# A two-layer decoder step on one NeuronCore: the queries' 1/rms multiplied into the low-rank rows, query evictions on ScalarE, four heads in turn

## Chip, core and metric

The kernel runs on one core of one Trainium2 chip. The metric is the device time of one execution in microseconds (us), the median of several runs; lower is better. The kernel before takes 2415.44 us (three runs, 2413.04 to 2415.65).

## What is computed

One inference step of a decoder of two layers, in float32, for 1024 prompt tokens and 64 sample tokens (8 sequences of 8), 1088 columns in all. The first layer mixes tokens by causal means. The second is attention with a compressed latent of 256 numbers and a rotary key of 64 per token. Each layer then has an MLP with squared ReLU and a gated add. The part that the change touches is how the queries of the second layer are made:

```python
def _rmsnorm(x, g):
    xf = x.astype(jnp.float32)
    y = xf * lax.rsqrt(jnp.mean(xf * xf, axis=-1, keepdims=True) + NORM_EPS)
    return (y * g.astype(jnp.float32)).astype(x.dtype)

def _mla_queries(u, pos, w_dq, q_norm, w_uq, w_uk):
    cq = _rmsnorm(u @ w_dq, q_norm)              # 384 numbers per token
    q = jnp.einsum('btr,rhe->bthe', cq, w_uq)    # 8 heads x (128 + 64)
    q_lat = jnp.einsum('bthn,rhn->bthr', q[..., :QK_NOPE], w_uk)
    return q_lat, _rope(q[..., QK_NOPE:], pos)
```

The factor 1/rms ("rstd") is one number per token. It can be multiplied into `cq` ahead of the product with `w_uq`, or into the product after it.

## The kernel before

Activations lie transposed, features on the 128 partitions and tokens along the columns, in three chunks of columns: chunk 0 and chunk 1 with 384 tokens, chunk 2 with 320 (256 prompt tokens and the 64 sample tokens). A float32 product is made of three matmuls: each operand is split into a rounded high half (a cast, on ScalarE, L146) and the remainder (a subtraction on VectorE, L147), and `mm3` (L188 to L190) adds high x high, high x low and low x high in one PSUM bank.

The order of the program is a list of steps that `Plan` collects and then runs; `add_late(n, fn)` puts a step behind the next n steps that use a weight piece. The weight pieces are loaded ahead on SP's queue (L168) through a ring of four. Each engine works through its own instructions in the order in which they are built, so an instruction that waits holds up all that stand behind it on its engine; a scheduler in the compiler may interleave neighbouring steps.

The stages are: pooling, first MLP, first gated add, `qkv_phase` (L662), attention, output projection, second MLP, second gated add. The change lies in `qkv_phase`, which works as follows.

- `krope` and `latent` make the rotary key and the latent of the three chunks.
- `qdown(c)` (L747) makes the 384 low-rank query rows of chunk c, three PSUM banks of 24 matmuls each; `split_scaled` multiplies by the gain of the norm and splits them. The squares are added up in the tile `acc` (L259).
- `low_rstd(c)` (L687) turns the sums of squares into the two rstd rows of a chunk, that of the latent and that of the queries: two matmuls with a column of ones (L694) give a row in PSUM, ScalarE copies it (L696), a DMA folds it over the partitions (L697, `ss`), VectorE finds 1/sqrt by three Newton steps (L699 to L705), a DMA writes the row to DRAM (L709, `row`), and a second one reads it back to all 128 partitions (L710, into `E["r"]`, a slab whose tile is called `hid`).
- `latent_end(c)` (L720) multiplies the latent by its rstd, stores and splits it.
- `qrope(g, c)` (L772) makes the rotary part of four heads from two banks of 9 matmuls each, with six VectorE operations (L781), two casts (L794) and two subtractions; four stores go to DRAM (L799, `q_d`). For g = 0 a step ahead of these multiplies the cosine and sine tables of the chunk by the queries' rstd (L784), so that the rotary part is scaled with them.
- `qnope(hh, c)` (L758) makes the other part of head hh from one bank of 9 matmuls. VectorE evicts it and multiplies by the rstd at once (L762), and SP stores it (L764, `qn_d`). In chunk 2 ScalarE copies the sample tokens aside (L768).

The heads come in pairs: heads 0 and 1 of all chunks, then 2 and 3, and so on; ahead of every fourth `qnope` stands one `qrope`. The attention that follows makes values and keys (tiles `vh`, `kh`, `one`), loads the queries back (L168 `raw<-qn_d`, L178 `q<-q_d`) and starts with the scores (L891, tile `s`).

Of the kernel before, what the change touches and what calls it, by code (L numbers as in the profile page):

```python
# [11 lines left out]
F32 = mybir.dt.float32  # L12
F32R = mybir.dt.float32r
I32 = mybir.dt.int32
AF = mybir.ActivationFunctionType
ALU = mybir.AluOpType
# [4 lines left out]
P = 128  # L21
# [23 lines left out]
CH = [(0, 384), (384, 384), (768, 320)]  # L45
NCH = len(CH)
# [66 lines left out]
def kernel(ctx: ExitStack, tc: tile.TileContext, io: dict):  # L113
    nc = tc.nc
# [15 lines left out]
    def gain(name):  # L130
        o, w = io["gain_at"][name]
        return gains[:, o:o + w]

    h = []
    qn_d = [dpool.tile([P, T], F32, name=f"qn_d{i}") for i in range(H)]
# [9 lines left out]
    def split(hi, lo, x):  # L145
        nc.scalar.copy(out=hi, in_=x)  # L146
        nc.vector.tensor_tensor(out=lo, in0=x, in1=hi.bitcast(F32), op=ALU.subtract)  # L147

    def split_scaled(hi, lo, x, g):
        nc.scalar.activation(hi, x, AF.Copy, scale=g)  # L150
        nc.vector.scalar_tensor_tensor(  # L151
            out=lo, in0=x, scalar=g, in1=hi.bitcast(F32), op0=ALU.mult, op1=ALU.subtract)
# [27 lines left out]
    plan = Plan(load_piece)  # L180
# [32 lines left out]
    def u_pair(c):  # L213
        n = CH[c][1]
        uh = S["u"].tile([P, n], F32R, tag=f"uh{c}", bufs=KT, name="uh")
        ul = S["u"].tile([P, n], F32R, tag=f"ul{c}", bufs=KT, name="ul")
        return uh, ul

    def slab():
        return S["hid"].tile([P, 2176], F32R, tag="hid", bufs=5, name="hid")  # L220
# [29 lines left out]
    def square(c, x, acc, add=None, new=None):  # L250

        n = CH[c][1]
        if acc is None:
            acc = S["tmp"].tile([P, n], F32, tag=f"acc{c}", bufs=1, name="acc") if new is None else new()
            nc.scalar.activation(acc, x, AF.Square)
        else:
            s = sq_tile(n)
            nc.scalar.activation(s, x, AF.Square)  # L258
            (add or nc.vector).tensor_tensor(out=acc, in0=acc, in1=s, op=ALU.add)  # L259
        return acc  # L260
# [57 lines left out]
    def lin(c, w, k, m, mo, src=None):  # L318
        n = CH[c][1]
        wh, wl = (x.rearrange("p (k m) -> p k m", k=k) for x in w)  # L320
        ps = bank()[:, :n]
        x = src or U[c]
        mm3(ps, [(wh[:, i, mo:mo + m], wl[:, i, mo:mo + m], x[i][0], x[i][1]) for i in range(k)])
        return ps
# [337 lines left out]
    def qkv_phase():  # L662
        E = {}
# [20 lines left out]
        def hl_tile(n):  # L684
            return S["hl"].tile([P, 384], F32, tag="hl", bufs=4, name="hl")[:, :n]

        def low_rstd(c):  # L687

            o, n = CH[c]
            p, m = small_shape(c)  # L690
            ss = tiny("ss", (p, 2 * m)).rearrange("p (k m) -> p k m", k=2)
            for k, (name, dim) in enumerate((("zz", KR), ("qq", QR))):
                ps = bank()[0:1, :n]
                nc.tensor.matmul(out=ps, lhsT=ones, rhs=E[name, c], start=True, stop=True)  # L694
                row = sq_tile(n)[0:1]
                nc.scalar.activation(row, ps, AF.Copy, scale=1.0 / dim)  # L696
                nc.scalar.dma_start(out=ss[:, k, :], in_=row)  # L697
            q = RC[c].unsqueeze(1).broadcast_to([p, 2, m])
            nc.vector.tensor_tensor(out=ss, in0=ss, in1=q, op=ALU.mult)  # L699
            nc.vector.tensor_tensor(out=ss, in0=ss, in1=q, op=ALU.mult)  # L700
            v = ss.rearrange("p k m -> p (k m)")
            nc.vector.tensor_scalar(out=v, in0=v, scalar1=EPS, scalar2=None, op0=ALU.add)
            y = rsqrt(v).rearrange("p (k m) -> p k m", k=2)
            nc.vector.tensor_tensor(out=y[:, 0], in0=y[:, 0], in1=RC[c], op=ALU.mult)
            nc.vector.scalar_tensor_tensor(  # L705
                out=y[:, 1], in0=y[:, 1], scalar=SCALE, in1=RC[c], op0=ALU.mult, op1=ALU.mult)
            row = dpool.tile([2, n], F32, name=f"row{S['rows']}")
            S["rows"] += 1
            nc.sync.dma_start(out=row.rearrange("k (p m) -> p k m", p=p), in_=y)  # L709
            nc.sync.dma_start(out=E["r"][:, :, o:o + n], in_=row.partition_broadcast(P))  # L710
# [9 lines left out]
        def latent_end(c):  # L720
            o, n = CH[c]
            r = E["r"][:, 0, o:o + n]
            g = gain("kv_norm")
            for i in range(2):
                z = E["z"][:, i, o:o + n]
                nc.vector.scalar_tensor_tensor(
                    out=z, in0=z, scalar=g[:, i:i + 1], in1=r, op0=ALU.mult, op1=ALU.mult)
                nc.sync.dma_start(out=io["latT"][i, :, o:o + n], in_=z)
                split(*[x[:, o:o + n] for x in S["cl"][i]], z)
# [17 lines left out]
        def qdown(c, *ws):  # L747
            pss = [lin(c, w, KT, P, 0) for w in ws]
            g = gain("q_norm")
            out = []  # L750
            for i, ps in enumerate(pss):
                uh, ul = u_pair(c)
                split_scaled(uh, ul, ps, g[:, i:i + 1])
                out.append((uh, ul))
                E["qq", c] = square(c, ps, E.get(("qq", c)))
            E["cq", c] = out

        def qnope(hh, c, w):  # L758
            o, n = CH[c]
            ps = lin(c, w, 3, P, (hh % 2) * P, E["cq", c])  # L760
            t = hl_tile(n)
            nc.vector.tensor_tensor(out=t, in0=ps, in1=E["r"][:, 1, o:o + n], op=ALU.mult)  # L762
            m = min(n, SEQ - o)
            nc.sync.dma_start(out=qn_d[hh][:, o:o + m], in_=t[:, :m])  # L764
            if m < n:
                if hh % 4 == 0:
                    E["qs"] = S["hl"].tile([P, 4, NS], F32, tag="qs", bufs=2, name="qs")
                nc.scalar.copy(out=E["qs"][:, hh % 4, :], in_=t[:, m:])  # L768
                if hh % 4 == 3:
                    nc.sync.dma_start(out=qns_d[hh // 4], in_=E["qs"])  # L770

        def qrope(g, c, w):  # L772

            o, n = CH[c]
            pss = [lin(c, w, 3, P, i * P, E["cq", c]) for i in range(2)]
            s = slab()[:, :5 * n].rearrange("p (k t) -> p k t", k=5)
            _, _, z1, t, x2 = (s[:, i, :].bitcast(F32) for i in range(5))
            cos, sin = (E["cs"][:, i, o:o + n] for i in range(2))

            def tt(out, a, b, op):  # L780
                nc.vector.tensor_tensor(out=out, in0=a, in1=b, op=op)  # L781

            if g == 0:
                nc.vector.tensor_tensor(  # L784
                    out=E["cs"][:, :, o:o + n], in0=E["cs"][:, :, o:o + n],
                    in1=E["r"][:, 1, o:o + n].unsqueeze(1).broadcast_to([P, 2, n]), op=ALU.mult)
            tt(z1, pss[0], cos, ALU.mult)
            tt(t, pss[1], sin, ALU.mult)
            tt(z1, z1, t, ALU.subtract)
            tt(t, pss[0], sin, ALU.mult)  # L790
            tt(x2, pss[1], cos, ALU.mult)
            tt(x2, x2, t, ALU.add)
            for z, hi in ((z1, 1), (x2, 3)):
                nc.scalar.copy(out=s[:, hi, :], in_=z)  # L794
                tt(s[:, hi + 1, :], z, s[:, hi, :].bitcast(F32), ALU.subtract)
            m = min(n, SEQ - o)
            v = s[:, 1:5, :].bitcast(F32)
            for i in range(4):
                nc.sync.dma_start(  # L799
                    out=q2_d[4 * g + i][:, o:o + m].rearrange("(q p) t -> p q t", q=4),  # L800
                    in_=v[32 * i:32 * i + 32, :, :m])
            if m < n:
                nc.sync.dma_start(out=qs_d[:, g * P:(g + 1) * P, :].rearrange("q p t -> p q t"), in_=v[:, :, m:])
# [7 lines left out]
        for c in range(NCH):  # L811
            plan.add(lambda *w, c=c: qdown(c, *w), *dq)
            plan.add_late(min(c + 1, 2), lambda c=c: low_rstd(c))
            plan.add_late(9, lambda c=c: latent_end(c))
        ropes = [(g, c) for g in range(2) for c in range(NCH)]
        nopes = [(hh, c) for j in range(4) for c in range(NCH) for hh in (2 * j, 2 * j + 1)]
        for i, (hh, c) in enumerate(nopes):
            if i % 4 == 0:
                g, cc = ropes.pop(0)
# [470 lines left out]
    mlp_phase(0)  # L1290
    ple_phase(0, lambda c: next_norm(c, None))
    qkv_phase()
    attention_phase()
    wo_phase()
# [124 lines left out]
```

## Time and profile before

| | us |
|---|---|
| median of three runs | 2415.44 |
| the profiled execution, its own time | 2413.58 |
| its span, first to last instruction | 2411.8 |
| TensorE (PE) busy | 2361.0 |
| VectorE (DVE) busy | 1226.1 |
| ScalarE (ACT) busy | 829.4 |
| mean granted TensorE clock, as a share of 2.4 GHz | 0.992 |

The profile page gives busy time by engine, the chain of work that ended last, and groups of instructions by source line. Matmuls overlap, so a busy PE says little of how fast it goes; gaps between the starts of matmuls, and the granted clock, say more. The part that the change touches runs from about 970 to 1097 us of the span, the attention from there to about 1410.

### The profile page before, as it was taken

Reading aid. Unit: us, or ns where it says so; the run is one execution under the profiler, and the core shown is the slowest. Engines: PE = TensorE matmul, PEld = TensorE weight load, DVE = VectorE, ACT = ScalarE, POOL = GpSimd, SP = SyncE. Lnnn points to the kernel's source line nnn. Section 1 sums busy time; section 2 is a strip of 40 time slices with the busy share of each in tenths; the row PEclk is TensorE's granted clock in tenths of the full one; section 3 lists DMA queues with packets and bytes.
Section 4 is the critical chain, followed back from the end, with each engine's and each line's share of the span. In section 5 each row is a group of like instructions: output and inputs, shape, how many; then the busy total and the mean of one; then the engine's idle time right before and its main releaser. Section 6 shows DMA issues by size and latency. Waiting matters only on the chain.

```text
span 2411.8 us, 35848 instructions
## 1 busy us (share of the span) xinstructions
PE 2361.0 (98%) x14516; PEld 2308.6 (96%) x14516; DVE 1226.1 (51%) x2406; ACT 829.4 (34%) x1557; POOL 11.0 (0%) x16
## 2 busy tenths in 40 slices
PE   7999999999999999998999999999999999999996
PEld 7999999999999999987988899999999999999996
DVE  5933333333333578477887765433333333334755
ACT  6622121121221444236777644312212212123432
POOL 0000000000000000000000000000000000000001
PEclk8999999999999999999999999999999999999998
DMA  8411111111111143257443351111111111111202
GB/s 269 125 55 44 44 45 44 44 44 47 49 47 44 40 124 130 58 153 223 149 126 125 94 200 55 52 47 49 44 44 44 44 44 44 44 44 44 64 27 78
DMA packets 97085, 186.53 MB, mean 77 GB/s; under 512 B 18633, under 2 KB 69001, under 8 KB 96144
## 3 DMA queue, kind: packets, MB, share of 16 engines
q1 hardware_dynamic: 90535, 179.78, 23.9%
q10 hardware_dynamic: 6384, 4.47, 0.6%
q8 instruction: 114, 1.87, 0.3%
q14 instruction: 52, 0.42, 0.1%
HBM read 155.00 MB, written 28.85 MB: 76 GB/s over the span
## 4 chain that ended last, share of the span: by engine, by line
PE 89%; DVE 4%; DMA 3%; ACT 2%; issue 1%; SPq 1%; ACTq 0%; DVEq 0%
PE mm L188 27%; PE mm L190 27%; PE mm L189 27%; PE s L891 2%; PE one L941 1%; PE one L1006 1%; PE one L918 1%; DMA craw<-in_cache 1%; PE mm L468 1%; ACT p L899 0%; PE mm L269 0%; DVE mx L898 0%; DVE hid L781 0%; PE one L188 0%; DMA hid<-row 0%
## 5 line engine op out<-in xcount | busy, mean ns | idle before, releaser
L188 PE MATMUL mm<-uh,whi 128*128 128x384 f32 (+1 forms) x2460 | 806.8, 328 | 12.8 <-ACT whi L146 5.9
L190 PE MATMUL mm<-uh,wlo 128*128 128x384 f32 (+1 forms) x2460 | 804.9, 327 | 0.2 <-DVE wlo L147 0.2
L189 PE MATMUL mm<-ul,whi 128*128 128x384 f32 (+1 forms) x2460 | 804.6, 327 | 0.0
L190 PE MATMUL mm<-hid,wlo 128*128 128x384 f32 (+1 forms) x1584 | 517.3, 327 | 0.0
L188 PE MATMUL mm<-hid,whi 128*128 128x384 f32 (+1 forms) x1584 | 517.1, 326 | 0.0
L189 PE MATMUL mm<-hid,whi 128*128 128x384 f32 (+1 forms) x1584 | 516.7, 326 | 0.0
L188 PEld LDWEIGHTS mm<-uh,whi 128*128 128x128 f32 x2460 | 464.0, 189 | 21.7 <-ACT whi L146 6.1
L190 PEld LDWEIGHTS mm<-uh,wlo 128*128 128x128 f32 x2460 | 463.9, 189 | 0.7 <-DVE wlo L147 0.7
L189 PEld LDWEIGHTS mm<-ul,whi 128*128 128x128 f32 x2460 | 464.0, 189 | 0.3 <-DVE ul L147 0.3
L146 ACT CAST whi<-raw 128x1024 fp32r<-128x1024 f32 (+3 forms) x184 | 190.9, 1038 | 753.1 <-PE mm L189 740.3
L314 DVE TENSOR_TENSOR h<-h,mm 128x384 f32<-128x384 f32 (+1 forms) x408 | 216.3, 531 | 422.2 <-PE mm L190 418.3
L188 PEld LDWEIGHTS mm<-hid,whi 128*128 128x128 f32 x1584 | 297.3, 188 | 3.8 <-issue 3.8
L190 PEld LDWEIGHTS mm<-hid,wlo 128*128 128x128 f32 x1584 | 297.3, 188 | 0.0
L189 PEld LDWEIGHTS mm<-hid,whi 128*128 128x128 f32 x1584 | 297.2, 188 | 0.0
L147 DVE TENSOR_TENSOR wlo<-raw,whi 128x1024 fp32r<-128x1024 f32 (+3 forms) x184 | 222.0, 1207 | 78.1 <-ACT whi L146 78.0
L557 DVE SCALAR_TENSOR_TENSOR t<-mm,r 128x384 f32<-128x384 f32 (+1 forms) x192 | 102.6, 535 | 299.4 <-PE mm L190 299.4
L559 ACT ACTIVATE t<-t 128x384 f32<-128x384 f32 (+1 forms) x192 | 97.0, 505 | 390.0 <-DVE t L557 390.0
L147 DVE TENSOR_TENSOR hid<-t,hid 128x384 fp32r<-128x384 f32 (+1 forms) x192 | 102.4, 534 | 140.4 <-ACT hid L146 140.4
L258 ACT ACTIVATE sq<-h 128x384 f32<-128x384 f32 (+1 forms) x126 | 63.2, 505 | 121.4 <-DVE h L314 60.2
L146 ACT CAST hid<-t 128x384 fp32r<-128x384 f32 (+1 forms) x192 | 95.0, 495 | 6.0
L259 DVE TENSOR_TENSOR acc<-acc,sq 128x384 f32<-128x384 f32 (+1 forms) x132 | 71.8, 544 | 42.3 <-ACT sq L258 41.5
L151 DVE SCALAR_TENSOR_TENSOR ul<-h,gains,uh 128x384 fp32r<-128x384 f32 (+1 forms) x96 | 54.0, 592 | 4.3 <-ACT uh L150 4.3
(206 smaller groups left out, 1944.6 us busy)
## 6 DMA issues: line engine op xcount, KB each, us to landing
raw<-in_w_up SPq DMA_DIRECT2D x64, 512.0 KB, 3.4
raw<-in_w_down SPq DMA_DIRECT2D x64, 512.0 KB, 3.5
craw<-in_cache SPq DMA_DIRECT2D x64, 192.0 KB, 2.7
raw<-in_w_gate SPq DMA_DIRECT2D x16, 512.0 KB, 3.5
craw<-in_cache SPq DMA_DIRECT2D x64, 128.0 KB, 2.1
h<-in_x_prompt SPq DMA_DIRECT2D x8, 512.0 KB, 6.7
raw<-qn_d SPq DMA_DIRECT2D x8, 512.0 KB, 3.5
q<-q_d SPq DMA_DIRECT2D x8, 512.0 KB, 4.8
```

Of the source, the lines that this page charges most:

```text
L146: nc.scalar.copy(out=hi, in_=x)
L147: nc.vector.tensor_tensor(out=lo, in0=x, in1=hi.bitcast(F32), op=ALU.subtract)
L151: nc.vector.scalar_tensor_tensor(out=lo, in0=x, scalar=g, in1=hi.bitcast(F32), op0=ALU.mult, op1=ALU.subtract)
L188: nc.tensor.matmul(out=out, lhsT=wh, rhs=xh, start=i == 0, stop=False)
L189: nc.tensor.matmul(out=out, lhsT=wh, rhs=xl, start=False, stop=False)
L190: nc.tensor.matmul(out=out, lhsT=wl, rhs=xh, start=False, stop=i == last)
L258: nc.scalar.activation(s, x, AF.Square)
L259: (add or nc.vector).tensor_tensor(out=acc, in0=acc, in1=s, op=ALU.add)
L314: nc.vector.tensor_tensor(out=h[c][:, dt, :], in0=h[c][:, dt, :], in1=ps, op=ALU.add)
L557: nc.vector.scalar_tensor_tensor(out=r, in0=ps, scalar=0.0, in1=R[c], op0=ALU.max, op1=ALU.mult)
L559: nc.scalar.activation(r, r, AF.Square)
L891: nc.tensor.matmul(out=st[:, a, :seg], lhsT=l[:, qs], rhs=r[:, ks], start=i == 0, stop=i == 4)
```

## The change

Five things change in `qkv_phase`.

- `qdown` keeps the gained low-rank rows whole, in float32 (one ScalarE operation each), and no longer splits them.
- A new step `qdown_end(c)` multiplies these three row tiles of a chunk by the queries' rstd (VectorE) and splits them (ScalarE cast, VectorE subtraction). It stands directly ahead of the first `qrope` for chunk 0, three steps later for chunk 1, eight for chunk 2.
- The multiplication by the rstd goes from the eviction in `qnope` and from the rotary tables in `qrope`.
- Evictions of heads 0 to 5 become plain copies on ScalarE and their stores are issued by ScalarE's queue; heads 6 and 7 stay on VectorE and SP.
- The heads come in two groups of four instead of four pairs.

```diff
--- before.py
+++ after.py
@@ -747,21 +747,27 @@
         def qdown(c, *ws):
             pss = [lin(c, w, KT, P, 0) for w in ws]
             g = gain("q_norm")
-            out = []
+            E["cq", c] = []
             for i, ps in enumerate(pss):
-                uh, ul = u_pair(c)
-                split_scaled(uh, ul, ps, g[:, i:i + 1])
-                out.append((uh, ul))
+                z = u_pair(c)[0].bitcast(F32)
+                nc.scalar.activation(z, ps, AF.Copy, scale=g[:, i:i + 1])
+                E["cq", c].append(z)
                 E["qq", c] = square(c, ps, E.get(("qq", c)))
-            E["cq", c] = out
+
+        def qdown_end(c):
+            o, n = CH[c]
+            for i, z in enumerate(E["cq", c]):
+                nc.vector.tensor_tensor(out=z, in0=z, in1=E["r"][:, 1, o:o + n], op=ALU.mult)
+                E["cq", c][i] = u_pair(c)
+                split(*E["cq", c][i], z)
 
         def qnope(hh, c, w):
             o, n = CH[c]
             ps = lin(c, w, 3, P, (hh % 2) * P, E["cq", c])
             t = hl_tile(n)
-            nc.vector.tensor_tensor(out=t, in0=ps, in1=E["r"][:, 1, o:o + n], op=ALU.mult)
+            (nc.scalar.copy if hh < 6 else nc.vector.tensor_copy)(out=t, in_=ps)
             m = min(n, SEQ - o)
-            nc.sync.dma_start(out=qn_d[hh][:, o:o + m], in_=t[:, :m])
+            (nc.scalar if hh < 6 else nc.sync).dma_start(out=qn_d[hh][:, o:o + m], in_=t[:, :m])
             if m < n:
                 if hh % 4 == 0:
                     E["qs"] = S["hl"].tile([P, 4, NS], F32, tag="qs", bufs=2, name="qs")
@@ -780,10 +786,6 @@
             def tt(out, a, b, op):
                 nc.vector.tensor_tensor(out=out, in0=a, in1=b, op=op)
 
-            if g == 0:
-                nc.vector.tensor_tensor(
-                    out=E["cs"][:, :, o:o + n], in0=E["cs"][:, :, o:o + n],
-                    in1=E["r"][:, 1, o:o + n].unsqueeze(1).broadcast_to([P, 2, n]), op=ALU.mult)
             tt(z1, pss[0], cos, ALU.mult)
             tt(t, pss[1], sin, ALU.mult)
             tt(z1, z1, t, ALU.subtract)
@@ -812,8 +814,10 @@
             plan.add(lambda *w, c=c: qdown(c, *w), *dq)
             plan.add_late(min(c + 1, 2), lambda c=c: low_rstd(c))
             plan.add_late(9, lambda c=c: latent_end(c))
+        for c in range(NCH):
+            plan.add_late((0, 3, 8)[c], lambda c=c: qdown_end(c))
         ropes = [(g, c) for g in range(2) for c in range(NCH)]
-        nopes = [(hh, c) for j in range(4) for c in range(NCH) for hh in (2 * j, 2 * j + 1)]
+        nopes = [(hh, c) for j in range(2) for c in range(NCH) for hh in range(4 * j, 4 * j + 4)]
         for i, (hh, c) in enumerate(nopes):
             if i % 4 == 0:
                 g, cc = ropes.pop(0)
```

The rows below are instructions as the built program holds them, in the order of one engine, without waits or times. The first place is TensorE's queue behind the last matmul of `qdown(2)`. In the names, `mm` with a number is one PSUM bank, `uh` and `ul` the halves of a low-rank row tile, `hl` and `acc` the sums of squares of the latent and of the queries. Before:

```order
L190 MATMUL mm_9202<-uh_8559,wlo_8920 128x320
L188 MATMUL mm_9265<-uh_9006,whi_8926 128x384
L189 MATMUL mm_9265<-ul_9007,whi_8926 128x384
L190 MATMUL mm_9265<-uh_9006,wlo_8927 128x384
...
L188 MATMUL mm_9275<-uh_9019,whi_8926 128x384
L189 MATMUL mm_9275<-ul_9020,whi_8926 128x384
L190 MATMUL mm_9275<-uh_9019,wlo_8927 128x384
L694 MATMUL mm_9302<-hl_8830,ones_63 1x384
L694 MATMUL mm_9307<-acc_9105,ones_63 1x384
L188 MATMUL mm_9332<-uh_9006,whi_9248 128x384
```

And now:

```order
L190 MATMUL mm_9196<-uh_8559,wlo_8920 128x320
L188 MATMUL mm_9271<-uh_9257,whi_8926 128x384
L188 MATMUL mm_9281<-uh_9257,whi_8926 128x384
L694 MATMUL mm_9307<-hl_8830,ones_63 1x384
L189 MATMUL mm_9271<-ul_9258,whi_8926 128x384
L190 MATMUL mm_9271<-uh_9257,wlo_8927 128x384
...
L189 MATMUL mm_9281<-ul_9268,whi_8926 128x384
L190 MATMUL mm_9281<-uh_9267,wlo_8927 128x384
L694 MATMUL mm_9312<-acc_9101,ones_63 1x384
L188 MATMUL mm_9337<-uh_9257,whi_9239 128x384
```

The first matmul behind `qdown(2)` read a tile of `qdown(0)` (uh_9006); now it reads one that `qdown_end(0)` writes (uh_9257). The two L694 matmuls are those of chunk 1 in both, and stand behind it in both.

The second place is VectorE's queue at the same time. L760 is the new multiplication by the rstd, L147 with `ul` the new subtraction, L787 what was L781 (rotary arithmetic), L726 and L147 with `c` belong to the latent, L699 begins the Newton steps of chunk 1. Before:

```order
L151 SCALAR_TENSOR_TENSOR ul<-mm,gains,uh 128x320
L784 TENSOR_TENSOR hid<-hid 128x2x384
L259 TENSOR_TENSOR acc<-acc,sq 128x320
L781 TENSOR_TENSOR hid<-mm,hid 128x384 x3
L781 TENSOR_TENSOR hid<-hid 128x384
L726 SCALAR_TENSOR_TENSOR hid<-hid,gains 128x384
L781 TENSOR_TENSOR hid<-mm,hid 128x384
L781 TENSOR_TENSOR hid<-hid 128x384 x2
L699 TENSOR_TENSOR ss<-ss,y 128x6
```

And now:

```order
L259 TENSOR_TENSOR acc<-acc,sq 128x320
L760 TENSOR_TENSOR uh<-uh,hid 128x384 x3
L147 TENSOR_TENSOR ul<-uh 128x384 x3
L726 SCALAR_TENSOR_TENSOR hid<-hid,gains 128x384 x2
L787 TENSOR_TENSOR hid<-mm,hid 128x384
L147 TENSOR_TENSOR c_8578<-hid,c_8577 128x384
L147 TENSOR_TENSOR c_8580<-hid,c_8579 128x384
L787 TENSOR_TENSOR hid<-mm,hid 128x384 x2
L787 TENSOR_TENSOR hid<-hid 128x384
L787 TENSOR_TENSOR hid<-mm,hid 128x384
L787 TENSOR_TENSOR hid<-hid 128x384 x2
L699 TENSOR_TENSOR ss<-ss,y 128x6
```

The addition for chunk 2's `acc` has moved ahead of the first operation that reads chunk 0's rstd (L784 then, L760 now).

The third place is the start of the attention. On SP's queue, before (L158 loads a weight piece of the sample path, `qn_d_71` is head 0, `qn_d_72` head 1, `q_d_79` the rotary part of head 0):

```order
L803 DMA qs_d<-hid 128x4x64
L158 DMA whole<-in_w_ukt 128x1024
L764 DMA qn_d_77<-hl 128x384
L764 DMA qn_d_78<-hl 128x384
L764 DMA qn_d_77<-hl 128x256
L764 DMA qn_d_78<-hl 128x256
L770 DMA qns_d_90<-qs 128x256
L158 DMA whole<-in_w_ukt 128x1024
L168 DMA raw<-qn_d_72 128x1024
L178 DMA q_9944<-q_d_79 128x1024
```

And now:

```order
L805 DMA qs_d<-hid 128x4x64
L168 DMA raw<-qn_d_71 128x1024
L770 DMA qn_d_77<-hl 128x256
L770 DMA qn_d_78<-hl 128x256
L776 DMA qns_d_90<-qs 128x256
L168 DMA raw<-qn_d_72 128x1024
L158 DMA whole<-in_w_ukt 128x1024 x2
L178 DMA q_9977<-q_d_79 128x1024
```

Head 0's load stood some 40 transfers ahead of the first of these rows before; now it stands behind all rotary stores. On ScalarE's queue, which casts the loaded queries (L146 `whi<-raw`) and the values (`vh`), the end of the stage now reads:

```order
L774 COPY qs<-hl 128x64 x3
L146 CAST whi<-raw 128x1024
L146 CAST vh<-one 128x256 x8
L146 CAST kh<-one 128x512 x3
L146 CAST whi<-raw 128x1024
```

The first of these two casts is head 0's; before, it stood ahead of the last rotary casts, and no cast of a load stood between the last copies and the eight of the values.

## Rows read from the trace of the kernel before

**Rows 1.** The page: span, and the chain that ended last by engine.

```profile
span 2411.8 us, 35848 instructions
...
PE 89%; DVE 4%; DMA 3%; ACT 2%; issue 1%; SPq 1%; ACTq 0%; DVEq 0%
```

**Rows 2.** Waits of TensorE, 1033 to 1115 us: total, times, longest.

```profile
PE mm L188 <- DVE hl L762: 2.4, 1, 2.4
PE s L891 <- DMA q<-q_d: 1.7, 1, 1.7
PE one L188 <- DVE hl L762: 0.7, 1, 0.7
...
PE mm L694 <- DVE acc L259: 0.5, 1, 0.5
```

**Rows 3.** Windows: length, busy of PE, PEld, DVE, ACT, POOL, granted clock, DMA, GB/s.

```profile
1033.00:1097.00 64.00, 60.17 (x344) 56.26 (x344) 50.25 (x125) 17.32 (x36) 0.00 (x0) 0.97 0.63 177
...
1055.00:1060.00 5.00, 2.64 (x11) 2.58 (x11) 3.19 (x7) 0.24 (x1) 0.00 (x0) 0.72 0.57 189
1060.00:1065.00 5.00, 5.00 (x30) 5.00 (x30) 5.00 (x12) 3.03 (x6) 0.00 (x0) 0.94 0.67 214
...
1110.00:1410.00 300.00, 288.38 (x2037) 259.75 (x2036) 240.96 (x487) 218.97 (x475) 0.00 (x0) 1.00 0.42 130
```

**Rows 4.** Timeline of TensorE: start, duration, instruction, idle before it.

```profile
1032.98 0.34 PE L188 MATMUL mm<-uh,whi 128*128 128x384 f32 x1
...
1036.84 0.81 PE L694 MATMUL mm<-acc,ones 128*1 128x384 f32 x2
...
1053.68 0.33 PE L190 MATMUL mm<-uh,wlo 128*128 128x384 f32 x1
...
1054.72 0.34 PE L190 MATMUL mm<-uh,wlo 128*128 128x384 f32 x1
1057.42 0.63 PE L188 MATMUL mm<-uh,whi 128*128 128x320 f32 x1 [2.36 <-DVE hl L762]
```

**Rows 5.** The chain of waits, 1020 to 1062 us: start, length, what.

```profile
1021.66 0.63 DVE ul L151
...
1030.21 4.07 DMA row<-y
1034.29 4.84 DMA hid<-row
1039.16 0.97 DVE hid L784
...
1044.87 2.46 DMA ss<-sq
...
1052.53 4.25 DMA hid<-row
```

**Rows 6.** Waits of all engines, 1033 to 1115 us.

```profile
ACT sq L696 <- DVE acc L259: 3.0, 1, 3.0
```

**Rows 7.** Groups by line and shape, 1033 to 1098 us: count, busy, mean ns, idle before.

```profile
L762 DVE TENSOR_TENSOR hl<-mm,hid 128x384 f32<-128x384 f32 x16 | 8.3, 551 | 3.7 <-DMA hid<-row 3.2 <-DMA qn_d<-hl 0.6
...
L794 ACT CAST hid<-hid 128x384 fp32r<-128x384 f32 x8 | 4.1, 511 | 7.2 <-DVE hid L781 7.0 <-DMA q_d<-hid 0.3
```

**Rows 8.** Line L717, a ScalarE copy out of PSUM: min, median, max ns.

```profile
L717 ACT COPY hid<-mm x6: 418/472/479, 978.9 to 996.7; 128x384 f32<-128x384 f32 x4, 128x320 f32<-128x320 f32 x2
```

**Rows 9.** Timelines of TensorE, SP and ScalarE at the attention's start.

```profile
1095.37 0.28 PE L190 MATMUL one<-whi,c 128*128 128x256 f32 x1
1096.37 0.39 PE L188 MATMUL one<-whi,c 128*128 128x256 f32 x1 [0.72 <-DVE hl L762]
...
1101.65 0.44 SPq L168 DMA_DIRECT2D raw<-qn_d  x1
...
1107.99 1.04 ACT L146 CAST whi<-raw 128x1024 fp32r<-128x1024 f32 x1 [1.59 <-DMA raw<-qn_d]
```

**Rows 10.** The page's DMA issues: count, KB each, median us to landing.

```profile
raw<-qn_d SPq DMA_DIRECT2D x8, 512.0 KB, 3.5
```

## The prediction

> **What bounds the kernel now.** I read the page first. The chain that ended last is 89% TensorE [rows 1], so a change pays only where TensorE stands still or runs slowly. Next I read TensorE's waits from the end of `qdown(2)` to the first scores [rows 2]. Four matter: 2.4 us for an eviction (L762), 0.7 us for the last evictions, when the attention takes over the PSUM banks, 0.5 us for a sum of squares, and 1.7 us for the first rotary queries. The windows [rows 3] show a fifth cost: around the 2.4 us wait the granted clock is 0.72 of 2.4 GHz over 5 us and 0.94 over the next 5 us. The chip grants 1.2 or 2.4 GHz, so this is a stretch at 1.2 GHz, and it loses 0.28 x 5 + 0.06 x 5 = 1.7 us of full-clock work. Then I followed the chain of waits back from that eviction [rows 5]. It is no slow VectorE but the rstd itself: two transfers for chunk 0 (4.07 and 4.84 us) bring it to VectorE at 1039.16, and chunk 1's lands at 1052.53 + 4.25 = 1056.8.
>
> What the reader is to see: TensorE began `qrope(0, 0)` at 1032.98 [rows 4], 6.2 us before the rstd was there, and was not held up, because only evictions needed it and eight banks could fill. That slack is what the change spends.
>
> **The change part by part.**
>
> *The new wait of chunk 0.* The first matmul behind `qdown(2)` now reads a tile that has been multiplied by the rstd and cast. So TensorE starts when the rstd is on VectorE (1039.16), plus one multiplication (0.55, as for the equally large one of L762 [rows 7]), plus one cast (0.51, L794 [rows 7]), plus about 0.1 for hops: 1040.3. Nothing can stand in, since `qdown(2)` is done and TensorE works in order. One thing gets earlier: VectorE's L151 (0.63 us) lies in the chain that leads to this rstd [rows 5] and is gone. That gives 1039.7, a stall of 6.7 us from 1032.98. Bounds: 7.3 without that gain; 4.7 if the small write of the row takes two us less than its 4.07. I stay near the upper one, as the same weight loads stand around it in SP's queue.
>
> *Slow clock behind it.* The wait is longer than the 2.4 us one, so I charge its 1.7 us [rows 3]. Lower bound 0 is excluded by that row; upper bound 3.4, twice as long a stretch.
>
> *The new wait of chunk 1.* What is queued behind the waiting matmul decides here: the L694 matmuls that sum chunk 1's squares. The second one ran at 1036.84 [rows 4]; now it runs behind the 18 matmuls of the first `qrope`. These take 18 x 0.173 = 3.1 us (six steps from 1053.68 to 1054.72 [rows 4]) plus 1.7 for the clock: 1039.7 + 4.8 = 1044.5. Before, chunk 1's rstd landed 1056.8 - 1036.8 = 20.0 us behind that matmul. Of these, 3.0 us were ScalarE waiting for a VectorE addition that stood behind the rstd multiply [rows 6]; it is moved ahead of it and goes. So 17.0 us: the rstd is there at 1061.5, and TensorE gets a tile at 1062.7 (plus 1.2 as above). It has run out by then: 1044.5, plus 1.9 for the remaining row sums and 36 x 0.173 = 6.2 for four heads, is 1052.6. Stall 10.1 us. Bounds: 13.1 if the 3.0 us don't go. From below, from the issue of the folding DMA (1044.87) to the landing took 11.9 us, and row sum, copy and issue add some 1.8: 13.7 instead of 17.0, which leaves 6.8. I take 10.1, as nine VectorE operations of the first `qrope` still stand ahead of chunk 1's Newton steps. Another 1.7 us of clock follow.
>
> *Chunk 2.* Its rstd lands with chunk 1's, and `qdown_end(2)` has 9 us of matmuls ahead of it: nothing.
>
> *VectorE relieved.* The 18 L762 moved are 12 x 0.55 + 6 x 0.48 = 9.5 us, the three table multiplies 2.7 us; L760 and the new subtractions about balance L151 and more. VectorE is busy 50.25 of 64 us [rows 3], but TensorE's waits for it are those above. I count the 2.4, 0.7 and 0.5 us and the 1.7 of clock as gone: -5.3 us. It can't be more, as rows 2 hold no more.
>
> *ScalarE loaded.* 18 copies at 0.47 [rows 8], nine casts at 0.51 and 18 issues at some 0.44 (an issue on SP [rows 9]) are 21 us on top of 17.3 of 64 [rows 3]. Per group of four heads and one `qrope` ScalarE has 4 x 0.91 + 2 x 0.51 = 4.7 us of work in 54 x 0.173 = 9.3 us of matmuls. Covered, also if the copies were twice as long.
>
> *Four heads in turn.* Weight pieces stay in the ring longer, so the load of head 0's queries moves behind the last rotary stores on SP, and its cast ahead of all eight value casts on ScalarE. `qrope(1, 2)` ends 36 x 0.147 = 5.3 us before the last head; VectorE and four stores bring the load's issue to about 1.4 us behind that end. It lands 3.5 us later [rows 10] or 6.3 (1101.65 to 1107.99 [rows 9]); cast and first value take 1.4. TensorE fills four banks in 2.8 us, then waits 3.5 to 6.3 us. I take 3.5, a median of eight. SP reaches the rotary load earlier than before, so the old 1.7 us wait goes: +1.8 net.
>
> **Sum.** 6.7 + 1.7 + 10.1 + 1.7 - 5.3 + 1.8 = +16.7 us. On the profiled execution (2413.58) that is 2430.3; this execution lies 1.9 below the median of the runs, so against that it is 2432. I say **2431**. A measurement can tell about 0.2% (4.8 us) from no change.
>
> **A rule against a row.** Rows 5 price the read-back of an rstd at 4.84 and 4.25 us. In the Trainium skill, "DMA: Bandwidth & Descriptors", the section "Anatomy of one DMA — SWDGE (gpsimd) path" fits a transfer, for those issued by GpSimd, as about 2.0 us plus its bytes over 436 GB/s; an estimate by it for 393 kB is 2.9 us. By it the two stalls would be 3.3 us shorter together and the sum +13.4. The rows are of these very transfers on SP's queue, behind loads and stores, so the sum goes by them.
>
> **Rivals.**
>
> *A third stall that bites (0.17).* The load of head 0 takes 6.3 us, and the wait at the attention's start brings a slow stretch too: +16.7 + 2.8 + 1.7 = 21, 2436. For it: the same load did take that long in that crowd [rows 9]. Against: the median of 3.5.
>
> *Short chains (0.11).* With 4.7 and 6.8 for the stalls and no wait at the attention's start: 4.7 + 1.7 + 6.8 + 1.7 - 5.3 - 1.7 = +8, 2423. For it: a less crowded SP queue, 18 stores lighter. Against: the rstd transfers stood behind weight loads and rotary stores, which stay.
>
> *The other side, faster (0.08; the same mechanism by half, no change, 0.06).* One mechanism: a relieved VectorE delivers the rstd before TensorE asks. Then only gains are left, -5.3 - 1.7 = -7, 2408. It decides at the point where chunk 0's rstd reaches VectorE by 1031.8 and chunk 1's 1.2 us before TensorE has worked off the four heads; no change is reached where both stalls together fall under some 7 us. Against it: 8.9 us of chunk 0's delay are two transfers with no engine in them [rows 5], and they start at 1030.21, about when they would have to be over. The attention's own idle time, 300 - 288.4 = 11.6 us [rows 3], could shift by a few us with the new order, but hardly by 17.
>
> **How the numbers follow.** The forecast (two stalls, 2425 to 2434) has 0.58. The range 2420 to 2443 takes in the short chains, the third stall, and the upper bounds of both waits and of the clock; it leaves out no change and faster, 0.14, and a little above. Slower by over 0.2%: 0.58 + 0.17 + 0.11 = 0.86; within 0.2% 0.06; faster 0.08.
>
> **What would show it.** TensorE's largest two waits should be for the cast of the new low-rank tiles, near 1033 (6 to 7 us) and near 1052 (7 to 13 us), each followed by a window with a clock well under 1. The wait for L762 should be gone, the first row sum of chunk 1 should run near 1044, and the first value cast should wait for head 0's load. I am wrong if TensorE runs on at 1033, or if the rstd of chunk 1 lands before 1052.

## The result, and the profile after

The changed kernel takes 2433.03 us (median of six runs, 2429.14 to 2440.38), the kernel before 2414.24 us (six runs, 2411.92 to 2416.38). The ratio is 1.0079, 95% interval 1.0069 to 1.0089: slower by 0.8%, as forecast (2431, range 2420 to 2443).

The page of the changed kernel, span and chain by engine, as [rows 1]:

```profile
span 2433.5 us, 35861 instructions
...
PE 90%; DVE 4%; DMA 3%; ACT 2%; issue 1%; SPq 0%; DVEq 0%; ACTq 0%
```

TensorE's waits from 1020 to 1136 us, which answer to [rows 2]; total, times, longest:

```profile
PE mm L188 <- ACT uh L146: 15.6, 2, 10.2
PE one L188 <- DVE vl L147: 6.1, 1, 6.1
PE s L895 <- ACT p L903: 0.7, 1, 0.7
```

The four old waits (evictions of L762, a sum of squares, the first rotary queries) are gone. In their place stand two waits for the cast of the new low-rank tiles, 5.4 and 10.2 us, and one of 6.1 us at the attention's start.

TensorE's timeline around the first of them, as [rows 4]:

```profile
1032.91 0.31 PE L190 MATMUL mm<-uh,wlo 128*128 128x320 f32 x1
1038.64 1.01 PE L188 MATMUL mm<-uh,whi 128*128 128x384 f32 x2 [5.42 <-ACT uh L146]
1039.58 1.44 PE L694 MATMUL mm<-hl,ones 128*1 128x384 f32 x2
...
1043.36 0.52 PE L190 MATMUL mm<-uh,wlo 128*128 128x384 f32 x1
...
1045.63 0.81 PE L694 MATMUL mm<-acc,ones 128*1 128x384 f32 x2
```

TensorE stands from the end of `qdown(2)` to 1038.64. Behind that its matmuls of 384 columns start 0.32 us apart (43.04, 43.36, 43.68), where 0.17 us is usual. Chunk 1's second row sum runs at 1045.63, 8.8 us later than before.

The chain of waits, as [rows 5], for chunk 0, chunk 1 and the attention's start; start, length, what:

```profile
1029.47 3.63 DMA row<-y
...
1033.11 4.35 DMA hid<-row
...
1037.48 0.57 DVE uh L760
...
1038.08 0.52 ACT uh L146
...
1053.01 6.50 DMA row<-y
...
1059.52 3.81 DMA hid<-row
...
1063.35 0.57 DVE uh L760
...
1111.48 5.47 DMA raw<-qn_d
1116.97 1.05 ACT whi L146
1118.05 1.23 DVE wlo L147
1119.28 0.34 DVE vl L147
```

Each new wait ends with the operations that the forecast named: rstd transfer, multiplication, cast; and at the attention's start head 0's load, its cast and the first value.

Windows behind the three waits, as [rows 3]:

```profile
1038.64:1045.64 7.00, 7.00 (x21) 5.03 (x22) 4.29 (x9) 2.29 (x5) 0.00 (x0) 0.57 0.19 63
...
1064.51:1069.51 5.00, 5.00 (x17) 4.64 (x18) 4.85 (x11) 2.27 (x5) 0.00 (x0) 0.59 0.24 82
1069.51:1107.98 38.47, 38.47 (x238) 38.47 (x237) 26.94 (x54) 14.66 (x34) 0.00 (x0) 1.00 0.62 166
...
1119.66:1131.66 12.00, 12.00 (x67) 11.04 (x67) 5.93 (x12) 5.26 (x10) 0.00 (x0) 0.85 0.45 156
```

The granted clock is 0.57, 0.59 and 0.85 behind them, and 1.00 in the stretch between. Lost to it: 0.43 x 7 = 3.0, 0.41 x 5 = 2.1, 0.15 x 12 = 1.8 us.

The terms of the sum, in us, each measured in the profiled execution:

| term | forecast | measured |
|---|---|---|
| wait for chunk 0's rstd | 6.7 | 5.4 |
| clock behind it | 1.7 | 3.0 |
| wait for chunk 1's rstd | 10.1 | 10.2 |
| clock behind it | 1.7 | 2.1 |
| old waits and clock gone | -5.3 | -5.3 |
| attention's start (new wait less the old 1.7) | +1.8 | 6.1 - 1.7 = +4.4 |
| clock behind it | 0 | 1.8 |
| sum | +16.7 | +21.6 |

The spans differ by 2433.5 - 2411.8 = 21.7 us, so nothing of size is missing. The profiled execution (2435.28) lies 2.25 us above the median of its runs and that of before (2413.58) 0.66 below; 21.7 - 2.9 = 18.8 is the difference of the medians.

### The profile page after: what moved, and what is told of

It is laid out like the page before. It is cut to its first block, busy times and chain, and to the rows that moved or that the text cites. A ratio compares the mean times of both kernels' runs of the same rounds, so it can differ in the third digit from the quotient of the medians.

```text
span 2433.5 us, 35861 instructions
## 1 busy us (share of the span) xinstructions
PE 2367.1 (97%) x14516; PEld 2314.5 (95%) x14516; DVE 1221.7 (50%) x2394; ACT 839.6 (35%) x1584; POOL 11.0 (0%) x16
## 4 chain that ended last, share of the span: by engine, by line
PE 90%; DVE 4%; DMA 3%; ACT 2%; issue 1%; SPq 0%; DVEq 0%; ACTq 0%
PE mm L188 27%; PE mm L189 27%; PE mm L190 27%; PE s L895 2%; PE one L945 2%; DMA craw<-in_cache 1%; PE one L922 1%; PE mm L468 1%; PE one L1010 1%; DMA row<-y 1%; PE one L1082 0%; PE one L188 0%; ACT p L903 0%; DVE mx L902 0%; PE mm L269 0%
## 5 line engine op out<-in xcount | busy, mean ns | idle before, releaser
L188 PE MATMUL mm<-uh,whi 128*128 128x384 f32 (+1 forms) x2460 | 807.9, 329 | 24.7 <-ACT uh L146 17.7
L146 ACT CAST whi<-raw 128x1024 fp32r<-128x1024 f32 (+3 forms) x184 | 190.9, 1037 | 756.8 <-PE mm L189 741.0
L147 DVE TENSOR_TENSOR wlo<-raw,whi 128x1024 fp32r<-128x1024 f32 (+3 forms) x184 | 222.1, 1207 | 86.2 <-ACT whi L146 85.9
L147 DVE TENSOR_TENSOR hid<-t,hid 128x384 fp32r<-128x384 f32 (+1 forms) x192 | 102.4, 533 | 140.3 <-ACT hid L146 140.3
L146 ACT CAST hid<-t 128x384 fp32r<-128x384 f32 (+1 forms) x192 | 95.0, 495 | 6.0
L151 DVE SCALAR_TENSOR_TENSOR ul<-h,gains,uh 128x384 fp32r<-128x384 f32 (+1 forms) x96 | 53.9, 591 | 4.3 <-ACT uh L150 4.3
```

Source lines behind the costliest of these rows:

```text
L151: nc.vector.scalar_tensor_tensor(out=lo, in0=x, scalar=g, in1=hi.bitcast(F32), op0=ALU.mult, op1=ALU.subtract)
L188: nc.tensor.matmul(out=out, lhsT=wh, rhs=xh, start=i == 0, stop=False)
```

## Experiments

Ratios are to the kernel before, with the 95% interval.

### The head order, taken out and alone

`e1_pairs`: the changed kernel with heads in pairs (and `qdown_end(2)` two steps earlier, which that order needs).

```diff
-        nopes = [(hh, c) for j in range(2) for c in range(NCH) for hh in range(4 * j, 4 * j + 4)]
+        nopes = [(hh, c) for j in range(4) for c in range(NCH) for hh in (2 * j, 2 * j + 1)]
```

> The changed kernel with its heads in pairs, as before. Theory (the order of heads makes the late load of head 0's queries, and the two early waits come from the rstd): the wait at the attention's start falls from 6.1 us to under 2; the first wait stays at 5 to 6; the second begins 18 x 0.173 = 3.1 us earlier, since two heads fewer stand ahead of chunk 1, and ends where it did: 13 us. Time 2429 to 2433. Rival (the load is late for the evictions and stores on ScalarE, whatever the order): the wait at the attention's start stays near 6 us, time 2435 to 2438.

Measured: 2427.55 us, ratio 1.0043 (1.0027 to 1.0060). TensorE's waits, 970 to 1135 us:

```profile
PE mm L188 <- ACT uh L146: 16.7, 2, 12.1
PE s L895 <- ACT p L903: 0.8, 2, 0.7
PE s L895 <- DMA q<-q_d: 0.8, 1, 0.8
```

The wait at the attention's start is gone and the second one 2 us longer (forecast 13), as the theory has it; the time is 1.5 us under its range.

`e2_four_only`: the kernel before with the opposite edit, heads four in turn and nothing else.

> The kernel before with nothing changed but the order of heads: four in turn. Theory (the order alone makes the third wait): a wait of 4 to 7 us for the load of head 0's queries at the attention's start, in place of the 0.7 and 1.7 us; the 2.4 us wait for the eviction of chunk 0 or 1 stays between 0 and 3: 2417 to 2421. Rival (order without effect as long as VectorE and SP do the evictions): 2412 to 2416.

Measured: 2422.88 us, ratio 1.0031 (1.0020 to 1.0042). The same view:

```profile
PE one L188 <- DVE vl L147: 5.7, 1, 5.7
PE mm L188 <- DVE hl L762: 3.7, 2, 3.1
PE one L188 <- DVE hl L762: 1.5, 2, 0.9
```

And the clock behind the third wait:

```profile
1106.93:1118.93 12.00, 12.00 (x61) 11.04 (x62) 5.33 (x12) 4.69 (x10) 0.00 (x0) 0.80 0.64 220
```

The third wait appears without any other part of the change. Its time is over the range for two reasons: the slow stretch behind that wait, 0.20 x 12 = 2.4 us, was not in it, and the old waits for L762 grew, from 3.1 to 5.2 us together. The order alone costs 0.31%, all the rest (e1) 0.43%; together 0.74 of the 0.79%, which is the whole as far as intervals of 0.1 to 0.2% can tell.

### The evictions

`e3_dve_evict`: the changed kernel with all evictions on VectorE, unscaled, and all stores on SP.

```diff
-            (nc.scalar.copy if hh < 6 else nc.vector.tensor_copy)(out=t, in_=ps)
+            nc.vector.tensor_copy(out=t, in_=ps)
...
-            (nc.scalar if hh < 6 else nc.sync).dma_start(out=qn_d[hh][:, o:o + m], in_=t[:, :m])
+            nc.sync.dma_start(out=qn_d[hh][:, o:o + m], in_=t[:, :m])
```

> The changed kernel with all evictions of queries back on VectorE and their stores back on SP, unscaled. Theory (the evictions' engine is off the path): the two early waits stay at 5 to 6 and 10 us; SP has 18 issues more, so the wait at the attention's start stays at 6 or grows by up to 3 us: 2432 to 2437. Rival (ScalarE's new work delays casts or stores and costs time): 2425 to 2430.

Measured: 2436.29 us, ratio 1.0077 (1.0060 to 1.0093), the same as the change. The two early waits are 14.8 us together (longest 9.8), those at the attention's start 5.8. Which engine evicts makes no difference that these runs can tell.

### The rstd itself

`e4_no_rstd`: a multiplication by the cosine table in place of the rstd. The queries are then not normalised; the run serves for its time alone.

```diff
-                nc.vector.tensor_tensor(out=z, in0=z, in1=E["r"][:, 1, o:o + n], op=ALU.mult)
+                nc.vector.tensor_tensor(out=z, in0=z, in1=E["cs"][:, 0, o:o + n], op=ALU.mult)
```

> The changed kernel with the low-rank rows multiplied by the cosine table, which is there long before, in place of the rstd; the queries are therefore not normalised, and all work and transfers of the rstd stay. Theory (the two early stalls and the half clock behind them are waits for the rstd): both go, 5.4 + 10.2 us, and with them the half-clock stretches, 2 to 3 us each: 2411 to 2414; the wait at the attention's start stays at 6. Rival (TensorE waits as much for VectorE's multiplications and ScalarE's casts of the new tiles): waits of 2 us or more stay in front of the first matmul of each chunk, 2418 to 2425.

Measured: 2416.60 us, ratio 1.0011 (0.9997 to 1.0024). No wait for the new tiles is left; the largest is

```profile
PE one L188 <- DVE vl L147: 6.7, 1, 6.7
```

So the multiplications and casts cost TensorE nothing when their factor is there in time, and the two early stalls are the rstd's lateness, with the 1.2 us of multiplication and cast that follow it. The time is 2.6 us over the range: I had not added up what stays, old waits -5.3, attention's start 6.7 - 1.7 = +5.0, clock behind it (0.87 over 12 us) +1.6, which makes +1.3 on before.

### Why chunk 1's rstd is late

`e5_early_sums`: the row sums of chunks 1 and 2 ahead of the blocked matmul.

```diff
-            plan.add_late(min(c + 1, 2), lambda c=c: low_rstd(c))
+            plan.add_late(1, lambda c=c: low_rstd(c))
```

> The changed kernel with the row sums of chunks 1 and 2 put ahead of the first matmul that waits for chunk 0's rstd. Theory (chunk 1's rstd is late because its sums are queued behind the blocked matmul): the sums run near 1033 us, 12 us earlier, the rstd lands near 1051, ahead of the end of the four heads near 1053, and the second wait falls from 10.2 to under 1 us: 2419 to 2423. The first wait stays at 5 to 6. Rival (the transfers on SP's queue set the landing, whenever the sums run): the second wait stays over 5 us, 2427 to 2433.

Measured: 2430.26 us, ratio 1.0055 (1.0039 to 1.0072). The second wait is 7.7 us. The sums ran at 1034.75, 10.9 us earlier, but the rstd was there only 4.05 us earlier (1059.30 instead of 1063.35). VectorE's timeline shows where the rest stayed; L699 begins chunk 1's Newton steps, L705 with 128x3 ends them:

```profile
1037.73 1.50 DVE L760 TENSOR_TENSOR uh<-uh,hid 128x384 f32<-128x384 f32 x3 [1.45 <-DMA hid<-row]
...
1040.61 0.16 DVE L699 TENSOR_TENSOR ss<-ss,y 128x6 f32<-128x6 f32 x1
...
1045.02 0.56 DVE L787 TENSOR_TENSOR hid<-mm,hid 128x384 f32<-128x384 f32 x1 [2.55 <-PE mm L190]
...
1050.61 0.15 DVE L705 SCALAR_TENSOR_TENSOR y<-y 128x3 f32<-128x3 f32 x1
```

The same two steps in the changed kernel, then e5's two transfers:

```profile
1049.07 0.17 DVE L699 TENSOR_TENSOR ss<-ss,y 128x6 f32<-128x6 f32 x1
...
1052.10 0.16 DVE L705 SCALAR_TENSOR_TENSOR y<-y 128x3 f32<-128x3 f32 x1
```

```profile
1051.08 4.08 DMA row<-y
...
1055.22 4.05 DMA hid<-row
```

The Newton steps began 5.9 us behind the sums (3.4 in the change) and then took 10.1 us instead of 3.2, for they stand in VectorE's order between rotary operations that wait for TensorE, whose granted clock was 0.55 over the 7 us from 1038.89. So they ended only 1.5 us earlier than in the change. The other 2.5 us of the gain came from the transfers, above all from the row, 4.08 instead of 6.50 us. Wait and time lie in the rival's range, but not for its reason: most of the 10.9 us was lost in VectorE's queue. This is read from the trace; no run moved the Newton steps alone.

`e6_sums_inside`: each chunk's sums between the first and second bank of the next chunk's `qdown`.

```diff
-            pss = [lin(c, w, KT, P, 0) for w in ws]
+            pss = [lin(c, ws[0], KT, P, 0)]
+            if c:
+                low_rstd(c - 1)
+            pss += [lin(c, w, KT, P, 0) for w in ws[1:]]
...
-            plan.add_late(min(c + 1, 2), lambda c=c: low_rstd(c))
+            if c == 2:
+                plan.add_late(1, lambda c=c: low_rstd(c))
```

> The changed kernel with each chunk's row sums run after the first of the three banks of the next chunk's low-rank rows (chunk 2's behind the first rotary step), 48 matmuls or 8 us earlier for chunk 0 and 20 us earlier for chunk 1. Theory (nothing but the time at which the rstd arrives makes the two early stalls): chunk 0's rstd lands near 1029.5, ahead of 1031.8, both stalls are under 1 us, the wait at the attention's start stays: 2411 to 2414. Rival (the write and read-back of the rstd, behind weight loads on SP's queue, take as long as those loads leave): the first stall stays at 2 to 5 us, 2416 to 2420.

Measured: 2416.28 us, ratio 1.0002 (0.9991 to 1.0012). TensorE's waits, then three places of VectorE's timeline and one of SP's:

```profile
PE mm L188 <- ACT uh L146: 4.2, 2, 3.3
PE mm L189 <- DVE ul L147: 1.1, 3, 0.5
```

```profile
1044.70 0.56 DVE L763 TENSOR_TENSOR uh<-uh,hid 128x384 f32<-128x384 f32 x1 [3.48 <-DMA hid<-row]
...
1046.12 0.15 DVE L699 TENSOR_TENSOR ss<-ss,y 64x10 f32<-64x10 f32 x1
...
1052.01 0.15 DVE L705 SCALAR_TENSOR_TENSOR y<-y 64x5 f32<-64x5 f32 x1
```

```profile
1070.85 0.33 SPq L168 DMA_DIRECT2D raw<-qn_d  x1
```

Chunk 0's rstd came at 1025.5 and its wait is gone, so the timing of the rstd does make the first stall. Two waits of 0.9 and 3.3 us stay, for chunks 1 and 2. Chunk 1's is the length of its own chain, 19.1 us from its sums (1025.65) to its rstd (1044.70). In chunk 2's VectorE's queue shows again: its sums ran at 1037.76, but its Newton steps stood behind the multiplication (L763 in this kernel) that waited for chunk 1's rstd until 1044.70, and ended at 1052.16. Then SP issued its read-back only at 1057.05, 4.9 us after its row, behind a rotary store. The time agrees with the rival's, for another reason. Unexpectedly the third wait is gone too, for the scheduler put head 0's load at 1070.85, 40 us ahead of its place in the change.

`e7_inside_ropes`: as e6, with the last three rotary steps earlier.

```diff
-            if i % 4 == 0:
+            if i in (0, 4, 8, 11, 14, 17):
```

> As the run with the sums inside the next chunk, and the last three rotary steps put three, six and nine heads... that is ahead of heads 11, 14 and 17 of the list instead of 12, 16 and 20, so that the last rotary weights leave the ring sooner and the load of head 0's queries is issued some 8 us ahead of the last head. Theory: the third wait also goes, 6.1 us and the slow stretch behind it: 2403 to 2408, faster than before. Rival (the load goes, but the denser rotary work holds up evictions on VectorE): a wait of 2 us or more for evictions among the last heads, 2409 to 2414.

Measured: 2414.98 us, ratio 1.0002 (0.9993 to 1.0012). A miss: the third wait had already gone in e6, and the two early ones stay (5.4 us), so the run says nothing of its own.

### The queue of the rstd transfers

`e10_pool`: the changed kernel, the two transfers of `low_rstd` issued by GpSimd.

```diff
-            nc.sync.dma_start(out=row.rearrange("k (p m) -> p k m", p=p), in_=y)
-            nc.sync.dma_start(out=E["r"][:, :, o:o + n], in_=row.partition_broadcast(P))
+            nc.gpsimd.dma_start(out=row.rearrange("k (p m) -> p k m", p=p), in_=y)
+            nc.gpsimd.dma_start(out=E["r"][:, :, o:o + n], in_=row.partition_broadcast(P))
```

> The changed kernel with nothing changed but the queue of the two rstd transfers: GpSimd in place of SP. There they took 3.63 and 4.35 us for chunk 0, and 6.50 and 3.81 for chunk 1, whose row was issued some 2 us after it was ready, behind a rotary store. Theory 1 (SP's queue and its order make a good part of both waits, and from GpSimd a row costs about 2.0 us and its read-back 2.9, as an estimate by the Trainium skill's page DMA: Bandwidth & Descriptors would have it): the first wait falls from 5.4 to 2 or 3 us, the second from 10.2 to about 3, 2420 to 2424. Theory 2 (the transfers cost about 8 us whatever the queue, and only the place behind the stores goes): the first wait stays at 5 to 6, the second falls to 6: 2427 to 2430. Rival (issue from GpSimd is slower): both waits longer, over 2433.

Measured: 2435.27 us, ratio 1.0083 (1.0066 to 1.0100), not to be told from the change. The chain of waits for chunk 1:

```profile
1054.31 6.34 DMA row<-y
...
1060.94 3.84 DMA hid<-row
```

With nothing ahead of it on its queue the row took 6.34 us, on SP 6.50. The first wait grew to 7.5 us, the second is 9.9. None of the three cases in full, nearest the last. (Chunk 1's row in the change was issued 0.75 us after the end of the Newton steps, 1052.26 to 1053.01, not the 2 us of my text, so there was little to gain.) The Trainium skill, "DMA: Bandwidth & Descriptors", section "Issuing engines are not separate DMA queues", says that transfers of all issuing engines run on the same DMA engines; these two rows agree. Its fit in "Anatomy of one DMA — SWDGE (gpsimd) path", 2.0 and 2.9 us here as estimates, does not hold in this stage: for the three rows 3.3 to 6.3 us were measured, for the read-backs 3.7 to 5.0.

`e9_inside_pool`: e6 with the same edit.

> The changed kernel with the sums inside the next chunk's low-rank rows, and the write and the read-back of each rstd row (L709, L710) issued by GpSimd, which has nothing else to do there, in place of SP. With the sums inside but SP's queue, chunk 1's two transfers took 3.55 and 4.61 us, and chunk 2's read-back was issued at 1057.05, 4.9 us after its row, behind rotary stores that waited for VectorE. Theory (what is left of the early waits, 4.2 and 1.1 us and their slow clock, is that queue): both waits fall under 1 us each, 2407 to 2411, faster than before. Rival (the transfers cost as much or more from GpSimd): the waits stay at 3 us or more, 2414 to 2420.

Measured: 2417.31 us, ratio 1.0012 (1.0002 to 1.0022), with 3.7 us of waits for the new tiles left. The rival held: the transfers cost about the same from either queue (rows 2.6 to 3.7 us, read-backs 3.7 to 4.7; on SP in e6 those of chunks 0 and 1 took 2.73 and 3.55, and 3.60 and 4.61).

`e13_inside_qpool`: e6 with the rotary stores issued by GpSimd, so that SP is free for the rstd.

```diff
-                nc.sync.dma_start(
+                nc.gpsimd.dma_start(
                     out=q2_d[4 * g + i][:, o:o + m].rearrange("(q p) t -> p q t", q=4),
...
-                nc.sync.dma_start(out=qs_d[:, g * P:(g + 1) * P, :].rearrange("q p t -> p q t"), in_=v[:, :, m:])
+                nc.gpsimd.dma_start(out=qs_d[:, g * P:(g + 1) * P, :].rearrange("q p t -> p q t"), in_=v[:, :, m:])
```

> The changed kernel with the sums inside the next chunk's low-rank rows, and the stores of the rotary parts (four per step, and that of the sample tokens) issued by GpSimd in place of SP. So chunk 2's read-back no longer stands behind rotary stores on SP, which cost the run with the sums inside a wait of 3.3 us and a stretch at half clock. Theory: chunk 2's wait is gone, chunk 1's of 1 to 2 us stays, none at the attention's start: 2409 to 2413, faster than before by 0.1 to 0.2% or the same. Rival (chunk 2's rstd is late by VectorE's Newton steps, which end at 1052, and two transfers of 4 us more): a wait of 1.5 us or more stays, 2413 to 2417.

Measured: 2415.55 us, ratio 1.0000 (0.9991 to 1.0009). Chunk 2's wait is 2.5 us: the rival. Its Newton steps end at 1054.3 and the transfers bring the rstd to 1061.8, 7.5 us later; in e6 it was 9.1 us (1052.16 to 1061.26), so the rotary stores on SP had cost some 1.6 us there. The profiled execution is the longest of the eleven (2418.97).

### The kernel before, with earlier sums

`e8_before_inside`: the edit of e6 in the kernel before, where the rstd still enters at the eviction.

> The kernel before with nothing changed but the place of the row sums, inside the next chunk's low-rank rows. Theory (the 2.4 us wait of before is the rstd of chunk 1): it goes with its slow stretch of 1.7 us, the waits at the attention's start stay: 2409 to 2412. Rival (VectorE, 50 of 64 us busy, sets that wait): 2413 to 2416.

Measured: 2413.34 us, ratio 0.9992 (0.9982 to 1.0001). The waits for evictions:

```profile
PE one L188 <- DVE hl L765: 4.3, 2, 2.8
...
PE mm L188 <- DVE hl L765: 0.4, 1, 0.4
```

The 2.4 us wait for the rstd is down to 0.4, as the theory has it; the time lies in the rival's range. What it gave came back as 4.3 us at the attention's start, which TensorE now reaches 1.9 us earlier (1092.93 instead of 1094.78), and as 1.2 us for a sum of squares.

`e12_before_inside_ropes`: e8 with the edit of e7.

> The kernel before with the row sums inside the next chunk's low-rank rows and the last three rotary steps ahead of heads 11, 14 and 17 of the list. With the sums alone the wait for the rstd was gone and 4.3 us of waits for evictions on VectorE (longest 2.8) stood at the attention's start, behind the last rotary step. Theory (the rotary work of VectorE stands ahead of those evictions): they fall under 1.5 us in all, 2409 to 2412. Rival (VectorE's total work in the stage sets the wait, wherever the rotary steps stand): 3 us or more stay, 2413 to 2415.

Measured: 2412.66 us, ratio 0.9990 (0.9981 to 0.9999). The wait did not fall but became one of 5.3 us. VectorE's timeline names its cause, which neither theory had:

```profile
1095.31 0.56 DVE L765 TENSOR_TENSOR hl<-mm,hid 128x384 f32<-128x384 f32 x1 [3.64 <-DMA qn_d<-hl]
```

The eviction waits for a buffer of `hl` (there are four) whose store has not landed. More buffers were not tried. This is the only version under the kernel before beyond its interval, and by 0.1%, less than what I said a measurement can tell.

## Why the prediction was right, point by point

- **What bounds it, and the first wait**: right. TensorE was held where the tile is read, until rstd, multiplication and cast were through. 5.4 us instead of 6.7, since the rstd reached VectorE at 1037.48: the row was issued 0.7 us earlier (L151 was worth 0.6) and both transfers were shorter (3.63 and 4.35 us against [rows 5]).
- **The second wait**: right in size, 10.2 against 10.1, by terms that erred alike, so that the match to 0.1 us is luck: the sums ran at 1045.63 (forecast 1044.5), the rstd landed 17.7 us behind (17.0), TensorE ran out 1.3 to 1.7 us later than said. Only the queries' sum stood behind the `qrope` matmuls, the latent's ran among them at 1039.58. The reason was half right. "What is queued behind the waiting matmul decides here" names the sums; in e5 these ran 10.9 us earlier, but the Newton steps ended 1.5 and the rstd came 4 us earlier, for the steps are queued on VectorE among rotary operations. The prediction names nine of these, but only as a reason not to go below 10.1.
- **Slow clock**: charged at 1.7 us a wait by a shorter wait's row; 3.0 and 2.1 measured, within the bounds of 0 to 3.4.
- **Chunk 2, VectorE relieved, ScalarE loaded**: right. No wait for chunk 2, no old wait left, and e3 shows that ScalarE's part is covered. The copies took 0.478 us as costed:

```profile
L768 ACT COPY hl<-mm 128x384 f32<-128x384 f32 x12 | 5.7, 478 | 16.7 <-PE mm L190 16.7
```

- **The attention's start**: right mechanism, mis-sized. "I take 3.5, a median of eight" was the step that failed: in that crowd the load took 5.47 us, nearer the 6.3 of [rows 9] of the same place. The other term, "cast and first value take 1.4", was short too: they took 2.7 (1116.97 to 1119.66), since VectorE's subtraction for the same load (1.23 us) stands ahead of the first value. And a slow stretch followed, 1.8 us, that the sum put at nothing. This is the first rival (2436); the profiled execution took 2435.28, the median lies between it and the forecast. That the median came within 2 us of 2431 is in part luck: the sum was 4.9 us short of the profiled execution (16.7 against 21.6), and the two profiled executions lie 2.9 us further apart than the medians.
- **The rule against the row**: by the fit of the Trainium skill's "DMA: Bandwidth & Descriptors" the sum was +13.4, by rows +16.7; the spans differ by 21.7, and the transfers from GpSimd (e10) cost as much as from SP.
- **Faster**: the first half of its condition, chunk 0's rstd by 1031.8, was met in e6 (1025.5); the second, on chunk 1, was missed by 0.9 us, and chunk 2's rstd, to which the prediction gave no wait, by 3.3. These waits and the slow clock behind them (0.82 and 0.84 over twice 5 us from 1045.86, 0.66 over 5 us from 1062.30, 3.4 us lost in all) ate the gain. Of such a version nothing faster than before was found.

## What to carry to other kernels

A factor that is applied at the eviction may arrive as late as the PSUM banks last; moved into the operand it must be there at the first matmul, so work out from the trace when it arrives and what TensorE has left to do by then. When an in-order engine waits for one chunk's factor, look for the small chain of the next chunk queued behind that wait, or among work that hangs on it, on every engine that the chain uses: with one link advanced (the sums, by 10.9 us) the queueing moved to the next (VectorE), and 1.5 us were left. And price a late load at the place where it will run, by the row from that crowd and not by the median of the page, with every operation that stands between it and what waits.

## What the runs showed of the hardware

- A row of 3 KB took 3.63 us and 6.50 us on SP in the same execution, and 6.34 us from GpSimd in the second case: the queue was not the cause. In the change four rotary stores had been issued in the 2.5 us ahead of the slow one, and in e10 four in the 2 us ahead of it and beside it; in e5, where one stood ahead, the row took 4.08 us. That the stores slowed it was not tried by itself.
- In the changed kernel each wait of TensorE cost 1.8 to 3.0 us more than its own length, by the granted clock behind it. The loss did not grow with the wait: 3.0 us behind 5.4, 2.1 behind 10.2, 1.8 behind 6.1.
